# Down projection of a SwiGLU FFN by seven block products in place of eight, with the FFN's pools laid out anew

## The chip, the cores and the metric

One core of one Trainium2 chip runs the whole kernel. The metric is the device time of one execution in microseconds (us); the time before is the median of three runs. The profile is one further execution, taken by the hardware profiler.

## What is computed

One decoder layer on 512 tokens of 1024 features: a norm, a mixing stage with two groups of heads, a projection with residual, then the FFN (2816 inner features) and a last norm. The change lies in the FFN:

```python
h = rmsnorm(x, norm_ffn_w[l])
x = x + (jax.nn.silu(h @ w_gate[l]) * (h @ w_up[l])) @ w_down[l]
...
return rmsnorm(x, final_norm_w)
```

All of it is float32. The kernel gets float32 accuracy out of the matmul type float32r by splitting each operand into a head (`hi`, the value rounded to float32r) and a rest (`lo`), and by three matmuls in place of one (`mm3`): hi times hi, hi times lo, lo times hi.

## The kernel before

**Stages.** The first 278 us or so hold the projections and the attention; the output projection (`project`) and the norm before the FFN (`ffn_norm`, `norm_turn`, `norm_keep`) end them. Then come 22 blocks of 128 inner features. `gate_up(f)` multiplies one block of the gate and one of the up weights with the normed tokens: per weight 8 feature rows by `mm3`, 24 matmuls of 128x512, into one PSUM bank each (tag `G`, 4 banks). `gate_act(f)` takes Silu of the gate bank on ScalarE (L653), multiplies it with the up bank on VectorE (L654), and splits the product into `act` head and rest (L76 on ScalarE, L73 on VectorE).

**Down projection before.** `FFN_GROUPS = (12, 10)`: after 12 blocks, and again after the last 10, the loop over `hf` (two halves of the 1024 output columns) takes weight units of two blocks by 512 columns, and multiplies them for four tiles of 128 tokens into four banks (tag `D`); a bank is added to the residual `x2` at L742 when its sum is whole. The four last units are done token tile by token tile, so that tiles end one after the other.

**Weights.** `load_raw` loads a unit of 512 KB (tag `wr`, 3 buffers) from SyncE's queue, `split` makes the head (`copy_a`, L76, ScalarE) and the rest (`sub`, L73, VectorE) in one buffer (tag `ws`, 4 buffers). Of a block both weights are split some two blocks ahead of their use.

**The end.** For each token tile `rstd_halves` sums squares of both column halves on ScalarE (L154) and adds them on VectorE (L156, L158), GpSimd takes the power (L159), and both halves are scaled (L748, L749, L751) and stored.

**Order.** Each engine works through its own list in order. A scheduler writes the lists when the kernel is built; waits between engines are by semaphores. `last_norm` holds the splits of block 1 behind the last norm's rest.

Of the kernel before, what the change touches and what calls it, by code (L numbers as in the profile page):

```python
# [32 lines left out]
FFN_GROUPS = (12, 10)  # L33
# [3 lines left out]
NBIG, NP, NRAW, NSPL, T4, T2 = 11, 3, 3, 4, 3, 4  # L37


@with_exitstack  # L40
def hybrid_gmlp_nsa_kernel(
# [63 lines left out]
    def mm3(ps, sh, sl, mh, ml, first, last):  # L105
        nc.tensor.matmul(ps, lhsT=sh, rhs=mh, start=first, stop=False)  # L106
        nc.tensor.matmul(ps, lhsT=sh, rhs=ml, start=False, stop=False)  # L107
        nc.tensor.matmul(ps, lhsT=sl, rhs=mh, start=False, stop=last)  # L108
# [181 lines left out]
    # compressed blocks: rows (parity, d), columns (head, block)  # L290
# [18 lines left out]
    # compression MLPs, a quarter of the first layer at a time  # L309
# [61 lines left out]
    # keys, values, queries  # L371
# [106 lines left out]
    # =================== attention ===================  # L478
# [10 lines left out]
    # output projection  # L489
# [29 lines left out]
    # scores, a head at a time; groups of four heads share a tile of probabilities  # L519
# [32 lines left out]
    # compressed branch  # L552
# [34 lines left out]
    # probabilities times values: units of 128 keys, four heads  # L587
# [59 lines left out]

    acts = []

    def gate_act(f):  # L650
        pg, b = gu.pop(f)[1], f if f < FFN_GROUPS[0] else f - FFN_GROUPS[0]
        sg = t2([P, S], F32, f"sg{f}")
        nc.scalar.activation(sg, pg[0], AF.Silu)  # L653
        nc.vector.tensor_tensor(out=sg, in0=pg[1], in1=sg, op=OP.mult)  # L654
        if b % 2 == 0:
            if b // 2 < NP:
                acts.append(bp.tile([P, 2, 2, S], F32R, tag="P", name=f"act{f}", bufs=NP))
            else:
                acts.append(b8([P, 2, 2, S], F32R, f"act{f}"))
        at = acts[-1][:, b % 2]  # L660
        copy_a(at[:, 0], sg)
        sub(at[:, 1], sg, at[:, 0])

    # gate and up, a block of 128 features; the first in two halves of the tokens
    gu = {}

    def gate_up(f, part=None):
        if not part:
            ws = [load_cols(w, 0, KD, f * P, P, f"w{'gu'[a]}{f}", spare=f == 0, behind=last_norm if f == 1 else None)
                  for a, w in ((0, w_gate), (1, w_up))]  # L670
            gu[f] = ws, [bank("G" if part is None else "S", [P, S], f"gu{f}{a}") for a in range(2)]
        cut = slice(0, S) if part is None else slice(part * 256, part * 256 + 256)
        for (hi, lo), z in zip(*gu[f]):
            for k in range(KD):
                mm3(z[:, cut], hi[:, k], lo[:, k], h2h[k // 4][:, k % 4, cut], h2l[k // 4][:, k % 4, cut],
                    k == 0, k == KD - 1)
# [29 lines left out]
    gate_up(0, 1)  # L706
    gate_act(0)
    zp.__exit__(None, None, None)

    # =================== FFN ===================  # L710
    fp = tc.tile_pool(name="ps_f", bufs=1, space=PSUM, reuse_waits="tile")
    ps = fp.__enter__()
    f0 = 0
    onw = None
    for gi, nb in enumerate(FFN_GROUPS):
        last_group = gi == len(FFN_GROUPS) - 1
        if gi > 0:
            acts.clear()
        for b in range(nb):
            f = f0 + b  # L720
# [5 lines left out]
        for hf in range(2):
            c = slice(hf * 512, hf * 512 + 512)
            pd = [bank("D", [P, 512], f"pd{gi}{hf}{t}") for t in range(NT)]
            units = [load_cols(w_down, (f0 + b) * P, 2, hf * 512, 512, f"wd{gi}{hf}{b}") for b in range(0, nb, 2)]
            tail = NSPL if last_group and hf == 1 else 1  # L730
            chunks = [[u] for u in range(len(units) - tail)] + [list(range(len(units) - tail, len(units)))]
            for us in chunks:
                for t in range(NT):
                    ts = slice(t * P, (t + 1) * P)
                    for u in us:
                        hi, lo = units[u]
                        for k in range(2):
                            b = 2 * u + k
                            at = acts[u][:, k]
                            mm3(pd[t], at[:, 0, ts], at[:, 1, ts], hi[:, k], lo[:, k], b == 0, b == nb - 1)  # L740
            for t in range(NT):
                nc.vector.tensor_tensor(out=x2[t][:, c], in0=pd[t], in1=x2[t][:, c], op=OP.add)  # L742
# [42 lines left out]
```

## Time and profile before

| | us |
|---|---|
| median of 3 runs | 641.55 (640.45 to 644.6) |
| span of the profiled execution, first to last instruction | 639.6 |
| TensorE busy in it | 620.8 |
| VectorE busy | 315.2 |
| ScalarE busy | 267.6 |

The profiled execution has no time of its own beside its span; the median is 1.95 us over the span. PE is TensorE's matmuls, DVE VectorE, ACT ScalarE, POOL GpSimd, SP SyncE with its DMA queue. Matmuls overlap each other, so the time of a stretch over the number of its matmuls tells their pace, not the duration of one.

### The profile page before, as it was taken

The numbers are of one execution on the slowest core, as the hardware profiler recorded it, in microseconds if no ns is written. First come the engines' busy times: TensorE is split into PE (matmuls) and PEld (weight loads), VectorE is DVE, ScalarE is ACT, GpSimd is POOL, SyncE is SP. The second block draws the span as 40 slices with busy tenths as digits, with TensorE's granted clock in tenths as the row PEclk, the third lists the DMA queues.
The fourth block names the chain that finished last, engine by engine and source line by source line (L and its number), as shares of the span: only waits on it lengthen the run. The fifth ranks groups of instructions, "written<-read, shape, count | busy, mean of one in ns | idle before, by whom it ended". The sixth has DMA issues, their size and how long they took to land.

```text
span 639.6 us, 7644 instructions
## 1 busy us (share of the span) xinstructions
PE 620.8 (97%) x2913; PEld 503.6 (79%) x2913; DVE 315.2 (49%) x563; ACT 267.6 (42%) x489; POOL 67.3 (11%) x113
## 2 busy tenths in 40 slices
PE   7999899999999999999999999999999999999995
PEld 5778788787777667898888888888888888888884
DVE  4752778557878886753333333323233333333422
ACT  5753367467757775442222222211122222222322
POOL 3100100015533650100000000000000000000001
PEclk8999999999999999999999999999999999999999
DMA  8451535451000211043333333333323333333202
GB/s 311 144 138 56 176 107 166 155 184 48 1 2 20 79 44 56 2 132 99 98 99 98 99 98 99 98 100 98 96 82 100 89 99 96 99 99 99 66 34 98
DMA packets 76628, 61.85 MB, mean 97 GB/s; under 512 B 3872, under 2 KB 64304, under 8 KB 76592
## 3 DMA queue, kind: packets, MB, share of 16 engines
q1 hardware_dynamic: 76016, 60.32, 31.0%
q10 hardware_dynamic: 576, 1.05, 0.4%
q8 instruction: 23, 0.38, 0.2%
q14 instruction: 13, 0.11, 0.1%
HBM read 59.27 MB, written 2.10 MB: 96 GB/s over the span
## 4 chain that ended last, share of the span: by engine, by line
PE 88%; DVE 4%; ACT 3%; DMA 2%; POOL 1%; issue 1%; SPq 0%; POOLq 0%; ACTq 0%; DVEq 0%
PE gu L107 13%; PE gu L108 13%; PE gu L106 12%; PE pd L108 6%; PE pd L106 6%; PE pd L107 6%; PE o L618 4%; PE ptp L603 3%; PE s L535 2%; PE po L107 2%; PE po L108 2%; PE po L106 2%; PE z_v L108 1%; PE z_v L106 1%; PE z_v L107 1%; PE z_q L108 1%
## 5 line engine op out<-in xcount | busy, mean ns | idle before, releaser
L106 PE MATMUL gu<-h2h,wg_s 128*128 128x512 f32 (+1 forms) x184 | 70.1, 381 | 0.2 <-ACT h2h L76 0.2
L107 PE MATMUL gu<-h2l,wg_s 128*128 128x512 f32 (+1 forms) x184 | 70.0, 380 | 0.2 <-DVE h2l L73 0.2
L107 PE MATMUL gu<-h2l,wu_s 128*128 128x512 f32 (+1 forms) x184 | 69.9, 380 | 0.0
L108 PE MATMUL gu<-h2h,wu_s 128*128 128x512 f32 (+1 forms) x184 | 69.9, 380 | 0.0
L106 PE MATMUL gu<-h2h,wu_s 128*128 128x512 f32 (+1 forms) x184 | 69.9, 380 | 0.0
L108 PE MATMUL gu<-h2h,wg_s 128*128 128x512 f32 (+1 forms) x184 | 69.9, 380 | 0.0
L106 PE MATMUL pd<-wd_s,act 128*128 128x512 f32 x176 | 68.5, 389 | 0.0
L107 PE MATMUL pd<-wd_s,act 128*128 128x512 f32 x176 | 68.5, 389 | 0.0
L108 PE MATMUL pd<-wd_s,act 128*128 128x512 f32 x176 | 68.5, 389 | 0.0
L73 DVE TENSOR_TENSOR wg_s<-wg_r,wg_s 128x1024 fp32r<-128x1024 f32 x22 | 27.2, 1236 | 78.4 <-ACT wg_s L76 78.3
L76 ACT ACTIVATE wu_s<-wu_r 128x1024 fp32r<-128x1024 f32 x26 | 27.5, 1061 | 78.0 <-issue 63.1
L73 DVE TENSOR_TENSOR wd_s<-wd_r,wd_s 128x1024 fp32r<-128x1024 f32 x22 | 27.0, 1225 | 67.3 <-ACT wd_s L76 67.3
L76 ACT ACTIVATE wd_s<-wd_r 128x1024 fp32r<-128x1024 f32 x22 | 23.3, 1059 | 71.2 <-PE pd L108 43.7
L653 ACT ACTIVATE sg<-gu 128x512 f32<-128x512 f32 x22 | 13.2, 598 | 80.7 <-PE gu L108 80.7
L654 DVE TENSOR_TENSOR sg<-gu,sg 128x512 f32<-128x512 f32 x22 | 15.2, 692 | 57.0 <-PE gu L108 57.0
L107 PEld LDWEIGHTS gu<-h2l,wg_s 128*128 128x128 f32 x184 | 34.6, 188 | 7.0 <-DVE h2l L73 0.4
L106 PEld LDWEIGHTS gu<-h2h,wg_s 128*128 128x128 f32 x184 | 34.6, 188 | 7.0 <-ACT h2h L76 0.5
L159 POOL TENSOR_TENSOR rstd_y<-s_y,mhalf 128x1 f32<-128x1 f32 x4 | 2.2, 549 | 359.5 <-DVE s_y L158 359.5
L108 PEld LDWEIGHTS gu<-h2h,wu_s 128*128 128x128 f32 x184 | 34.6, 188 | 6.6
L107 PEld LDWEIGHTS gu<-h2l,wu_s 128*128 128x128 f32 x184 | 34.6, 188 | 6.6
L108 PEld LDWEIGHTS gu<-h2h,wg_s 128*128 128x128 f32 x184 | 34.6, 188 | 6.5
L106 PEld LDWEIGHTS gu<-h2h,wu_s 128*128 128x128 f32 x184 | 34.6, 188 | 6.4
(264 smaller groups left out, 1280.1 us busy)
## 6 DMA issues: line engine op xcount, KB each, us to landing
wg_r<-in_w_gate_dram SPq DMA_DIRECT2D x22, 512.0 KB, 3.9
wu_r<-in_w_up_dram SPq DMA_DIRECT2D x22, 512.0 KB, 3.7
wd_r<-in_w_down_dram SPq DMA_DIRECT2D x22, 512.0 KB, 3.7
wo_r<-in_w_o_dram SPq DMA_DIRECT2D x8, 512.0 KB, 4.3
x_sb<-in_x_dram SPq DMA_DIRECT2D x4, 512.0 KB, 9.1
wv_r<-in_w_in_dram SPq DMA_DIRECT2D x4, 512.0 KB, 7.7
wu_r<-in_w_in_dram SPq DMA_DIRECT2D x4, 512.0 KB, 3.7
w1k_r<-in_cmp_k_w_dram SPq DMA_DIRECT2D x4, 512.0 KB, 3.9
```

What stands on the lines that cost most here:

```text
L73: return (eng or nc.vector).tensor_tensor(out=o, in0=a, in1=hi.bitcast(F32), op=OP.subtract)
L76: return nc.scalar.activation(o, a, AF.Copy)
L106: nc.tensor.matmul(ps, lhsT=sh, rhs=mh, start=first, stop=False)
L107: nc.tensor.matmul(ps, lhsT=sh, rhs=ml, start=False, stop=False)
L108: nc.tensor.matmul(ps, lhsT=sl, rhs=mh, start=False, stop=last)
L159: nc.gpsimd.tensor_tensor(out=r, in0=ms[:, 1:2], in1=mhalf, op=OP.pow)
L535: nc.tensor.matmul(sb, lhsT=q, rhs=KAB[kv][:, a, b0:b0 + nbr, :n], start=(a == 0), stop=(a == 1))
L603: nc.tensor.transpose(pt[:rows, hh], src, ident)
L618: nc.tensor.matmul(o.rearrange("p h c -> p (h c)"), lhsT=v, rhs=PTs[u][:rows, a], start=(first and a == 0), stop=(last and a == 1))
L653: nc.scalar.activation(sg, pg[0], AF.Silu)
L654: nc.vector.tensor_tensor(out=sg, in0=pg[1], in1=sg, op=OP.mult)
```

## The change

Groups are now of 6, 6, 6 and 4 blocks. In a group, the blocks go in pairs (e = 0, 1). A pair's activations are four quarters: block e by half of the tokens; its down weights (256 rows by 1024 columns) are four quarters too: block e by half of the columns. The 2x2 by 2x2 product of quarters is done with seven products, M1 to M7, each on 2 token tiles (c) of 128: the operands of four of them are sums and differences of quarters, and banks `A`, `B`, `C` (two each) collect them; bank A goes through M1, M6, M7 and M4 and is added to a quarter of `x2` after each of them. A group's three pairs (two in the last) add into the same banks.

```diff
-FFN_GROUPS = (12, 10)
+FFN_GROUPS = (6, 6, 6, 4)
+NHALF, NDOWN = 8, 3
...
-    NB = {**dict(zip("MSTO", BANKS)), "G": 4, "D": 4}
+    NB = {**dict(zip("MSTO", BANKS)), "G": 2, "A": 2, "B": 2, "C": 2}
...
-    def split(raw, shape, name, eng=None, spare=False, behind=None):
+    def split(raw, shape, name, eng=None, spare=False, behind=None, halves=False):
...
+        elif halves:
+            hi = wp.tile([P, *shape], F32R, tag="wh", name=f"{name}_h", bufs=NHALF)
+            lo = wp.tile([P, *shape], F32R, tag="wh", name=f"{name}_l", bufs=NHALF)
...
     def gate_act(f):
+        pg, e = gu.pop(f)[1], f % 2
+        if e == 0:
+            raw_act[0] = t4([P, 4, 256], F32, f"sg{f}")
+        sg = raw_act[0]
+        own = sg[:, 2 * e:2 * e + 2].rearrange("p a c -> p (a c)")
+        nc.scalar.activation(own, pg[0], AF.Silu)
+        nc.vector.tensor_tensor(out=own, in0=pg[1], in1=own, op=OP.mult)
+        if e == 0:
+            return
+        ss = t4([P, 4, 256], F32, f"ss{f}")
+        ah, al = act_tile(f"ah{f}"), act_tile(f"al{f}")
+        copy_a(ah[:, 0:3], sg[:, 1:4])
+        for o, x, y, op in ((ss[:, 0], sg[:, 0], sg[:, 2], OP.add), (ss[:, 2], sg[:, 1], sg[:, 0], OP.subtract),
+                            (ss[:, 1], ss[:, 0], sg[:, 1], OP.subtract), (ss[:, 3], sg[:, 3], ss[:, 1], OP.subtract)):
+            nc.vector.tensor_tensor(out=o, in0=x, in1=y, op=op)
+        sub(al[:, 0:3], sg[:, 1:4], ah[:, 0:3])
+        copy_a(ah[:, 3:7], ss)
+        sub(al[:, 3:7], ss, ah[:, 3:7])
+        acts.append((ah, al))
...
     gate_up(0, 1)
+    for p in reversed(first_pools):
+        p.__exit__(None, None, None)
+    wp = ctx.enter_context(tc.tile_pool(name="weights_f", bufs=2, reuse_waits="tile"))
+    tp = ctx.enter_context(tc.tile_pool(name="temps_f", bufs=2, reuse_waits="tile"))
...
+    def down(gi, pairs):
+        raws = []
+        for p in pairs:
+            r = wp.tile([P, 2, 2, 512], F32, tag="wd", name=f"wd{p}_r", bufs=NDOWN)
+            nc.sync.dma_start(r, w_down[2 * p * P:(2 * p + 2) * P].rearrange("(e p) (h c) -> p e h c", p=P, h=2))
+            raws.append(r)
...
+        def product(name, slot, tag, first, src, before=None):
+            ws = []
+            for q, r in enumerate(raws):
+                if before:
+                    before(r)
+                w = wp.tile([P, 2, 512], F32R, tag="wh", name=f"wd{pairs[q]}{name}", bufs=NHALF)
+                b = src(r)
+                copy_a(w[:, 0], b)
+                sub(w[:, 1], b, w[:, 0])
+                ws.append(w)
+            for c in range(2):
+                if first:
+                    banks[tag, c] = bank(tag, [P, 512], f"p{tag}{gi}{c}")
+                z, ts = banks[tag, c], slice(c * P, (c + 1) * P)
+                for q, w in enumerate(ws):
+                    ah, al = acts[q]
+                    mm3(z, ah[:, slot, ts], al[:, slot, ts], w[:, 0], w[:, 1],
+                        first and q == 0, q == len(ws) - 1, not first)
...
+        product("M1", 0, "A", True, lambda r: r[:, 0, 0])
+        for c in range(2):
+            accumulate(2 + c, 0, banks["A", c])
+        product("M5", 3, "C", True, lambda r: r[:, 0, 0], diffs)
+        for c in range(2):
+            accumulate(c, 1, banks["C", c])
+        product("M6", 4, "A", False, lambda r: r[:, 0, 0], t2_of)
...
+        product("M2", 2, "B", True, lambda r: r[:, 1, 0])
+        product("M7", 5, "A", False, lambda r: r[:, 0, 1])
+        product("M3", 6, "C", False, lambda r: r[:, 1, 1])
+        product("M4", 1, "A", False, lambda r: r[:, 1, 0], t4_of)
+        for c in range(2):
+            accumulate(c, 0, banks["A", c])
...
-    for t in range(NT):
-        y = t4([P, DM], F32, f"y{t}")
+    for t in (2, 3, 0, 1):
+        y = b8([P, DM], F32, f"y{t}")
         r = rstd_halves(x2[t], y, f"y{t}")
```

`accumulate(t, hf, src)` adds a bank to a half of the columns of `x2[t]` on VectorE (128x512). `diffs(r)` is one VectorE subtraction of 128x1024 in place, `t2_of` and `t4_of` one of 128x512 each. A group's down weights now come as whole pairs of 1 MB (tag `wd`, 3 buffers). The first pools are closed before block 0's activation, and new pools take their memory.

How the lists stand now, at three places.

VectorE around the start of the first down projection. Before, `sg` is the Silu product of the last block, `wd_s` a weight unit, `act` the activation's rest, and `x_...<-pd` the addition to the residual:

```order
L654 TENSOR_TENSOR sg_3445<-gu_3396,sg_3445 128x512
L73 TENSOR_TENSOR wd_s<-wd_r,wd_s 128x1024
L73 TENSOR_TENSOR act_3382<-sg_3445,act_3382 128x512
L73 TENSOR_TENSOR wd_s<-wd_r,wd_s 128x1024 x5
L742 TENSOR_TENSOR x_0_1171<-pd_3450,x_0_1171 128x512
L742 TENSOR_TENSOR x_0_1171<-pd_3451,x_0_1171 128x512
```

Now, where wd0 to wd2 with M and a number are the weights of pairs 0 to 2 for one product (the first two here are M6's of pairs 0 and 1, wd2M_3174 is M6's of pair 2), `ss` the sums of quarters, and `al` the activation's rest:

```order
L675 TENSOR_TENSOR sg_3016<-gu_3032,sg_3016 128x512
L76 TENSOR_TENSOR wd0M_3166<-wd_r,wd0M_3166 128x512
L683 TENSOR_TENSOR ss_3083<-sg_3016 128x256
L76 TENSOR_TENSOR wd1M_3170<-wd_r,wd1M_3170 128x512
L683 TENSOR_TENSOR ss_3083<-ss_3083,sg_3016 128x256
L76 TENSOR_TENSOR al_3085<-sg_3016,ah_3084 128x768
L683 TENSOR_TENSOR ss_3083<-sg_3016,ss_3083 128x256
L76 TENSOR_TENSOR wd2M_3174<-wd_r,wd2M_3174 128x512
L748 TENSOR_TENSOR x_1_1172<-pA_3109,x_1_1172 128x512
L76 TENSOR_TENSOR al_3085<-ss_3083,ah_3084 128x1024
L748 TENSOR_TENSOR x_1_1172<-pA_3119,x_1_1172 128x512
```

The weight rests of a later product, three sums and the first addition to the residual now stand among the steps that the last pair's activations go through.

VectorE at the end of the program. Before, the last three additions and what stands behind them (`s_y`, `rstd_y` and `y` belong to the last norm of a token tile):

```order
L742 TENSOR_TENSOR x_1_1172<-pd_4626,x_1_1172 128x512
L158 TENSOR_TENSOR s_y_4803<-s_y_4803 128x1
L751 SCALAR_TENSOR_TENSOR y_4803<-x_1_1172,rstd_y_4808,onw 128x512
L742 TENSOR_TENSOR x_1_1172<-pd_4627,x_1_1172 128x512
L158 TENSOR_TENSOR s_y_4817<-s_y_4817 128x1
L751 SCALAR_TENSOR_TENSOR y_4816<-x_1_1172,rstd_y_4821,onw 128x512
```

Now, from the last addition on (tiles come in the order 2, 3, 0, 1; y_5057 is tile 3, y_5070 tile 0, y_5083 tile 1):

```order
L748 TENSOR_TENSOR x_0_1171<-pA_4905,x_0_1171 128x512
L166 TENSOR_TENSOR s_y_5058<-s_y_5058 128x1
L827 TENSOR_TENSOR y_5057<-x_1_1172,onw 128x512
L830 SCALAR_TENSOR_TENSOR y_5057<-x_1_1172,rstd_y_5062,onw 128x512
L164 TENSOR_SCALAR s_y_5071<-s_y_5071 128x1
L827 TENSOR_TENSOR y_5070<-x_0_1171,onw 128x512
L166 TENSOR_TENSOR s_y_5071<-s_y_5071 128x1
L164 TENSOR_SCALAR s_y_5084<-s_y_5084 128x1
L827 TENSOR_TENSOR y_5083<-x_0_1171,onw 128x512
L830 SCALAR_TENSOR_TENSOR y_5070<-x_0_1171,rstd_y_5075,onw 128x512
L166 TENSOR_TENSOR s_y_5084<-s_y_5084 128x1
L830 SCALAR_TENSOR_TENSOR y_5083<-x_0_1171,rstd_y_5088,onw 128x512
```

Behind the last addition there stood two rows, and now there stand eleven: three products with the norm's weight (L827), three scalings (L830) and five small rows of 128x1.

SyncE's queue around the first FFN weights. Before:

```order
L84 DMA wg_r<-in_w_gate_dram 128x8x128
L84 DMA wu_r<-in_w_up_dram 128x8x128
L84 DMA wg_r<-in_w_gate_dram 128x8x128
L84 DMA wu_r<-in_w_up_dram 128x8x128
L84 DMA wg_r<-in_w_gate_dram 128x8x128
L112 DMA onw<-in_final_norm_w_dram 128x1024
```

Now, from the same row on:

```order
L87 DMA wg_r<-in_w_gate_dram 128x8x128
L87 DMA wu_r<-in_w_up_dram 128x8x128
L120 DMA onw<-in_final_norm_w_dram 128x1024
L87 DMA wg_r<-in_w_gate_dram 128x8x128
L87 DMA wu_r<-in_w_up_dram 128x8x128
L87 DMA wg_r<-in_w_gate_dram 128x8x128
L756 DMA wd_r<-in_w_down_dram 128x2x1024
```

The last norm's weight (`onw`) has moved ahead of the loads of blocks 1 and 2, and the first pair of down weights stands behind them.

On TensorE the list is the same up to block 1 and has 66 matmuls of 128x512 fewer from there on; on VectorE it has 702 rows in place of 521, on ScalarE 398 in place of 328.

## Rows read from the trace of the kernel before

**Rows 1.** The page, its span and part 1: busy time, share, instructions.
```profile
span 639.6 us, 7644 instructions
...
PE 620.8 (97%) x2913; PEld 503.6 (79%) x2913; DVE 315.2 (49%) x563; ACT 267.6 (42%) x489; POOL 67.3 (11%) x113
```

**Rows 2.** The chain that ended last, around the FFN: start us, us, engine, tile, line.
```profile
278.60 0.39 PE gu L107
632.59 0.70 DVE x L742
```

**Rows 3.** Busy time of each engine from block 1 to the last matmul.
```profile
284.20:632.60 348.40, 348.36 (x1538) 288.12 (x1536) 118.31 (x135) 93.30 (x121) 1.65 (x3) 1.00 0.32 95
```

**Rows 4.** Groups by shape, 278 to 636 us: count | busy us, mean ns.
```profile
L106 PE MATMUL pd<-wd_s,act 128*128 128x512 f32 x176 | 68.5, 389 | 0.0
...
L106 PE MATMUL gu<-h2h,wg_s 128*128 128x512 f32 x168 | 65.4, 389 | 0.0
...
L73 DVE TENSOR_TENSOR wd_s<-wd_r,wd_s 128x1024 fp32r<-128x1024 f32 x22 | 27.0, 1225 | 67.3 <-ACT wd_s L76 67.3
...
L76 ACT ACTIVATE wd_s<-wd_r 128x1024 fp32r<-128x1024 f32 x22 | 23.3, 1059 | 71.2 <-PE pd L108 43.7 <-issue 27.5
...
L654 DVE TENSOR_TENSOR sg<-gu,sg 128x512 f32<-128x512 f32 x22 | 15.2, 692 | 57.0 <-PE gu L108 57.0
L73 DVE TENSOR_TENSOR act<-sg,act 128x512 fp32r<-128x512 f32 x22 | 15.1, 685 | 0.0
L76 ACT ACTIVATE act<-sg 128x512 fp32r<-128x512 f32 x22 | 13.6, 617 | 0.0
...
L742 DVE TENSOR_TENSOR x<-pd,x 128x512 f32<-128x512 f32 x16 | 10.7, 687 | 12.1 <-PE pd L108 12.1
```

**Rows 5.** Groups by shape, VectorE, whole span: one of 256 columns.
```profile
L572 DVE TENSOR_TENSOR sc<-ptc,cmask 128x256 f32<-128x256 f32 x4 | 1.7, 419 | 1.8 <-PE ptc L568 1.8
```

**Rows 6.** Timeline, VectorE, end of the first down half: start us, us [idle before].
```profile
433.55 1.28 DVE L742 TENSOR_TENSOR x<-pd,x 128x512 f32<-128x512 f32 x2
435.39 0.69 DVE L742 TENSOR_TENSOR x<-pd,x 128x512 f32<-128x512 f32 x1 [0.56 <-PE pd L108]
```

**Rows 7.** Timeline, VectorE, two scalings in a row.
```profile
273.24 1.42 DVE L166 SCALAR_TENSOR_TENSOR xf<-x,rstd_f,fwb 128x512 f32<-128x512 f32 x2 [0.66 <-POOL rstd_f L159]
```

**Rows 8.** Timeline, SyncE's queue, the last loads before the FFN.
```profile
247.01 0.37 SPq L84 DMA_DIRECT2D wg_r<-in_w_gate_dram  x1
274.68 0.34 SPq L112 DMA_DIRECT2D onw<-in_final_norm_w_dram  x1
```

**Rows 9.** DMA issues: count, KB each, median us to landing.
```profile
x_sb<-in_x_dram SPq DMA_DIRECT2D x4, 512.0 KB, 9.1
...
x<-in_x_dram SPq DMA_DIRECT2D x4, 512.0 KB, 6.8
```

**Rows 10.** Timeline, TensorE, the first matmul of block 1.
```profile
284.21 0.40 PE L106 MATMUL gu<-h2h,wg_s 128*128 128x512 f32 x1
```

**Rows 11.** Timeline, all engines, the end of the program.
```profile
632.17 0.39 PE L108 MATMUL pd<-wd_s,act 128*128 128x512 f32 x1
632.59 0.69 DVE L742 TENSOR_TENSOR x<-pd,x 128x512 f32<-128x512 f32 x1 [2.32 <-PE pd L108]
633.32 0.63 ACT L154 ACTIVATE y<-x 128x512 f32<-128x512 f32 x1 [3.07 <-DVE x L742]
...
634.07 0.16 DVE L158 TENSOR_TENSOR s_y<-s_y 128x1 f32<-128x1 f32 x1 [0.79 <-ACT y L154]
634.38 0.55 POOL L159 TENSOR_TENSOR rstd_y<-s_y,mhalf 128x1 f32<-128x1 f32 x1 [4.89 <-DVE s_y L158]
...
634.96 0.75 DVE L751 SCALAR_TENSOR_TENSOR y<-x,rstd_y,onw 128x512 f32<-128x512 f32 x1 [0.73 <-POOL rstd_y L159]
635.71 0.37 ACTq L750 DMA_DIRECT2D out_dram<-y  x1
```

More of the change, by code (lines that the diff above doesn't have):

```diff
@@ L55, in hybrid_gmlp_nsa_kernel @@
     bp = ctx.enter_context(tc.tile_pool(name="big", bufs=NBIG))
-    wp = ctx.enter_context(tc.tile_pool(name="weights", bufs=2))
-    tp = ctx.enter_context(tc.tile_pool(name="temps", bufs=3))
-    sp = ctx.enter_context(tc.tile_pool(name="small", bufs=4))
+    first_pools = [tc.tile_pool(name="weights", bufs=2), tc.tile_pool(name="temps", bufs=3),
+                   tc.tile_pool(name="small", bufs=4)]
+    wp, tp, sp = [p.__enter__() for p in first_pools]
     def b8(shape, dt, name):
         return bp.tile(shape, dt, tag="b8", name=name)
+    n_t4 = T4
     def t4(shape, dt, name):
-        return tp.tile(shape, dt, tag="t4", name=name, bufs=T4)
+        return tp.tile(shape, dt, tag="t4", name=name, bufs=n_t4)
     def t2(shape, dt, name):
@@ L103, in after, with mm3 @@
                           mybir.DependencyInfo(mybir.DependencyClass.NoSync, mybir.DependencyReason.DATA), reason="order")
[L105 to L108, printed above, removed]
+    def mm3(ps, sh, sl, mh, ml, first, last, more=False):
+        nc.tensor.matmul(ps, lhsT=sh, rhs=mh, start=first, stop=False, skip_group_check=more)
+        nc.tensor.matmul(ps, lhsT=sh, rhs=ml, start=False, stop=False, skip_group_check=more)
+        nc.tensor.matmul(ps, lhsT=sl, rhs=mh, start=False, stop=last, skip_group_check=more)
     def bcast_row(vec, n, name, tag=None):
@@ L648, in hybrid_gmlp_nsa_kernel, with act_tile @@
     acts = []
-    def gate_act(f):
[L651 to L662, printed above, removed]
+    n_act = [0]
+    raw_act = [None]
+    def act_tile(name):
+        n_act[0] += 1
+        if (n_act[0] - 1) % 8 < NP:
+            return bp.tile([P, 7, 256], F32R, tag="P", name=name, bufs=NP)
+        return b8([P, 7, 256], F32R, name)
+    def gate_act(f):
+        pg, e = gu.pop(f)[1], f % 2
[17 more added lines that the diff above has]
+        acts.append((ah, al))
     gu = {}
@@ L668, in gate_up @@
         if not part:
-            ws = [load_cols(w, 0, KD, f * P, P, f"w{'gu'[a]}{f}", spare=f == 0, behind=last_norm if f == 1 else None)
+            ws = [load_cols(w, 0, KD, f * P, P, f"w{'gu'[a]}{f}", spare=f == 0, behind=last_norm if f == 1 else None,
+                            halves=f > 0)
                   for a, w in ((0, w_gate), (1, w_up))]
@@ L706, in hybrid_gmlp_nsa_kernel @@
     gate_up(0, 1)
+    for p in reversed(first_pools):
+        p.__exit__(None, None, None)
+    wp = ctx.enter_context(tc.tile_pool(name="weights_f", bufs=2, reuse_waits="tile"))
+    tp = ctx.enter_context(tc.tile_pool(name="temps_f", bufs=2, reuse_waits="tile"))
+    sp = ctx.enter_context(tc.tile_pool(name="small_f", bufs=4, reuse_waits="tile"))
+    n_t4 = 2
     gate_act(0)
@@ L715, in hybrid_gmlp_nsa_kernel @@
     for gi, nb in enumerate(FFN_GROUPS):
[L716 to L720, printed above, removed]
+        acts.clear()
+        for f in range(f0, f0 + nb):
             if f > 0:
@@ L723, in hybrid_gmlp_nsa_kernel @@
                 gate_act(f)
-        if last_group:
+        if gi == len(FFN_GROUPS) - 1:
             onw = bcast_row(final_norm_w, DM, "onw", tag="wb")
[L726 to L732, printed above, removed]
-                for t in range(NT):
[L734 to L742, printed above, removed]
+        down(gi, range(f0 // 2, (f0 + nb) // 2))
         f0 += nb
-    for t in range(NT):
-        y = t4([P, DM], F32, f"y{t}")
+    for t in (2, 3, 0, 1):
+        y = b8([P, DM], F32, f"y{t}")
         r = rstd_halves(x2[t], y, f"y{t}")
```

28 lines of the change are left out of this document (24 added, 4 removed).

## Prediction

> **What bounds the kernel now.** I read the page's busy times first: TensorE is busy for 620.8 of 639.6 us, VectorE for 315.2 and ScalarE for 267.6 [rows 1]. The chain of waits then shows where that matters: from 278.60 it stays on TensorE's gate and up products and the down products and leaves them at 632.59 for the last norm [rows 2]. The windows give the stage's pace: from block 1's first matmul to the last one's end 348.40 us, all of them busy [rows 3]. Those are 6 x 168 gate and up matmuls and 3 x 176 down matmuls [rows 4], 1536 in all, so 348.40 / 1536 = 226.8 ns each; the 389 ns of a single one hold its overlap with the next. VectorE works for 118.31 us there, ScalarE for 93.30 [rows 3]. So in this stage a matmul less is 226.8 ns less, as long as operands come in time, and VectorE is a third used.
>
> **Matmuls removed.** Before, 22 blocks x 4 token tiles x 2 column halves x 3 = 528. Now a pair takes 7 products x 2 tiles x 3 = 42, and 11 pairs 462. 66 x 226.8 ns = 15.0 us, certain by the lists. Gate and up stay.
>
> **VectorE's new work in a down projection.** For a group of three pairs: 21 weight rests of 128x512, at 685 ns like the activation's (14.4 us); 3 differences of 128x1024 at 1225 (3.7); 6 of 128x512 (4.1); 14 additions at 687 (9.6) [rows 4]. That is 31.8 us, while TensorE needs 126 x 0.2268 = 28.6. But by the list 6 rests, 3 wide and 3 narrow differences (9.9 us) stand ahead of the last block's Silu product, under gate and up matmuls. In their place come the last pair's own steps: product 0.69, four sums of 128x256 at 0.42 [rows 5], rests of 768 columns (0.96, between 685 and 1225 ns) and 1024 (1.23), 4.6 in all; and the next block's two weight rests, 2.5. So 29.0 at full price. Two independent rows back to back take 1.28 us, not 1.37 [rows 6], which over some 40 rows is 3 us less: about 26. Between 26 and 29 against 28.6 is tight, but not late; I take the row of pairs, as most neighbours in the list are independent. ScalarE has 21 heads at 0.62 [rows 4] and is not near.
>
> [...]
>
> **Start of a down projection.** Call 0 the start of M1's first matmul. The last up matmul ends at about 0.16 (it started 0.23 before and lasts 0.39), and the product of Silu and up is done at about 0.9. Ahead of the copy of the activation's head on ScalarE stand the heads of M6's weights for pairs 0 and 1, whose buffers are those of the last block's up weight (a ring of eight, two blocks long), so they start only as this block ends: 2 x 0.62, until 1.1. The head of 768 columns (0.84, between 617 and 1059) is done at 1.9 to 2.3. TensorE reaches it after 8 matmuls, at 1.8: 0.1 to 0.5 us late. The rest of 768 columns comes, by VectorE's list, behind two weight rests and two sums: 3.7 to 4.1, and is wanted 8 matmuls later, at 3.8 to 4.1. The rest of 1024 follows after a sum, a weight rest and an addition: 6.5 to 7.0, wanted by the 29th matmul at 6.5 to 6.8. So 0.1 to 0.7 us for a group; I take 0.4, as the steps are late by about as much as the overlap of rows takes off. Four groups: 1.6 us. Before, the first chunk hid these steps: VectorE's last activation rest had 24 matmuls of other units ahead of it.
>
> Later products are fed: M6's last addition stands at about 14.5 in VectorE's list at full price, its bank is wanted for M7's second tile at about 19; M4's last weight rest is done at 23.5 and wanted at 26.5. The next block's weights are done at 26.6, wanted at 29.2. This holds with additions waiting for their bank as in the row of 0.56 us [rows 6].
>
> **The end.** Before, from the last matmul's end at 632.56 (632.17 and 0.39) the addition, square, power and scaling take until 635.71: 3.15 us [rows 11]. Now tiles 0 and 1 both end with M4, 3 matmuls apart, and VectorE, behind M4's last weight rest and tile 2's and 3's rows, has just finished the last addition but one when the last matmul ends. Behind it stand: scaling 0.67 (half of 1.42 [rows 7]), addition 0.60, small 0.11, product 0.60, scaling 0.67, small 0.11, product 0.60, two small 0.22, product 0.60, scaling 0.67, small 0.15, power 0.55 with 0.1 of handing over on either side, scaling 0.75: 6.5 us. So the tail is 3.4 us longer; 2.4 if VectorE is a microsecond ahead, 5 at full price with waits for the power.
>
> **The front.** The last norm's weight now stands ahead of block 1's loads on SyncE's queue. It waited until 274.68 in the trace, for the buffer that the FFN norm's weight leaves, while the loads up to 247.01 were long out [rows 8]. So block 1's gate weight leaves at 275.1. Queued loads of 512 KB landed in 6.8 us (four together) and 9.1 (at the start of the program) [rows 9]; as the second of four I take 5.5 to 6.8, that is by 281.9. Head 1.06 and rest 1.23 make 284.2; block 1 starts at 284.21 [rows 10], and its third matmul, at 284.66, is the first to want the rest. Cost 0; if it took the 9.1, 2 us.
>
> G has two banks instead of four: Silu frees the gate bank 0.6 us after the last gate matmul, plus a head of 1.06 ahead of it on ScalarE, and the next block wants it after 24 up matmuls, 5.4 us. No cost. The down loads of 1 MB a pair move the same bytes as before, a block or more ahead.
>
> **Sum.** -15.0 + 1.6 + 3.4 + 0 = -10.0 us on the profiled execution, 639.6 to 629.6. On the median, 1.95 over that span, 641.55 - 10.0 = 631.6.
>
> **Rivals.** First, nearly all of the gain stays: the starts cost 0.1 each, and the bare addition of tile 1 sets the tail, 1 us longer. 641.55 - 15.0 + 0.4 + 1.0 = 628.0. The lists speak for it, TensorE's rows of M1 to M6 being interleaved in the last group; eleven rows behind the last addition speak against it.
>
> Second, VectorE paces the down projection, and the kernel gets slower. In its list additions that wait for TensorE stand ahead of weight rests that TensorE wants two products on, and bank A must be read before M6, M7 and M4 may write it. At full price (29.0) plus five of the 14 additions waiting 0.6 us [rows 6], a group takes 32.0 in place of 28.6; the last one, with 16.5 + 4.6 at full price and 2 of waits, 23 in place of 19.0. That is 3 x 3.4 + 4 = 14.2 us: with the starts and the tail 641.55 - 15.0 + 14.2 + 1.6 + 3.4 = 645.8. It decides from the point where VectorE's list is 3 to 4 us later than I have it; at half of that the time is 638.7. A third of use in the whole stage [rows 3] speaks against it, the down stage's own 26 to 29 of 28.6 for it.
>
> [...]
>
> Third, the front or the two G banks hold up TensorE: if Silu or the product came 5.4 us late, each further us would cost 21 us over 21 blocks; the front alone 2. About 636 with a front of 2 us and a stall of 2 to 3 elsewhere.
>
> **How the numbers follow.** Forecast 0.60, range 629 to 634 (starts 0.4 to 2.8, tail 2.4 to 5); first rival 0.14; second 0.18, a good half of it at the half way of 638.7; third 0.08. Since unknown costs lie mostly above, the range is 627.5 to 639.5. A difference of 1%, 6.4 us, is about what can be told: faster means below 635.1. From the forecast nearly all, the first rival, and a little of the others: 0.76; same 0.19; slower 0.05.
>
> **What would show it.** In the profile after: 1470 matmuls from block 1 on at 226.8 ns; at each group's start TensorE idle in two or three gaps of 0.1 to 0.5 us, released by ScalarE's head or VectorE's rest of the activations; no gaps later in a group; between the last matmul and the last scaling 6 to 7 us of VectorE; block 1 not waiting for a DMA. Wrong it would be if TensorE waited for weight rests or additions in the middle of a group, or if the tail stayed at 3 us.

## The result and the profile after

| | before | after |
|---|---|---|
| median, us | 641.61 (640.45 to 644.6, 4 runs) | 631.36 (630.81 to 632.05, 4 runs) |
| ratio | | 0.9835, 95% interval 0.9813 to 0.9857 |
| span of the profiled execution, us | 639.6 | 629.2 |
| block 1's first matmul to the last one's end, us | 348.35 | 335.00 |
| from there to the end of the last scaling, us | 3.15 | 7.27 |

The forecast was 631.6. One of the executions of `e2_vector_one` below ran at a lower granted clock (0.85, 684.01 us) and is left out of its median. The two lower lines of the table come from the timeline: before, 284.21 to 632.56, and on to 635.71 [rows 10, 11]; after, 282.81 to 617.81, and on to 625.08.

The page's span and busy times of the changed kernel answer to [rows 1]:

```profile
span 629.2 us, 7754 instructions
...
PE 606.5 (96%) x2847; PEld 489.9 (78%) x2847; DVE 411.3 (65%) x735; ACT 298.7 (47%) x544; POOL 68.1 (11%) x113
```

VectorE works 96 us more than before, in 172 rows more, TensorE 14 us less. The windows show where that stands. Columns: stretch, then busy us and count for PE, PEld, DVE, ACT and POOL, then the granted clock, DMA share and GB/s. The stretches are the whole stage (as [rows 3]), the first group's down projection, the last group's, and the end:

```profile
282.81:617.81 335.00, 335.00 (x1472) 275.06 (x1470) 212.55 (x299) 122.74 (x172) 0.55 (x1) 1.00 0.31 95
337.24:365.90 28.66, 28.66 (x126) 23.31 (x125) 26.14 (x40) 13.99 (x20) 0.00 (x0) 1.00 0.31 106
598.04:617.81 19.77, 19.77 (x85) 15.30 (x83) 18.85 (x34) 9.92 (x21) 0.55 (x1) 1.00 0.00 0
617.81:629.20 11.39, 0.00 (x0) 0.00 (x0) 5.72 (x14) 4.82 (x10) 2.47 (x3) 0.66 0.49 184
```

Read three things in them. The granted clock is 1.00 of full speed over the stage, and in both down projections. The stage holds 1470 matmuls (the window counts two more, which block 0 began and which still run at its left edge, as in [rows 3]); at 226.8 ns each they need 333.4 us, and 1.6 us are left for waits. And VectorE, a third used over the stage before, is busy for 26.14 of 28.66 us in a three-pair group and for 18.85 of 19.77 in the last one. The 40 rows of the three-pair group last 29.0 us when their durations are added up one by one; neighbours overlap, and so the engine is busy for 26.14.

The durations that the sum took from neighbours [rows 4, 5] can now be read as they are, in the groups by shape of the stage (count | busy us, mean ns):

```profile
L748 DVE TENSOR_TENSOR x<-pA,x 128x512 f32<-128x512 f32 x31 | 21.2, 688 | 4.1 <-PE pA L116 3.7
...
L76 DVE TENSOR_TENSOR al<-sg,ah 128x768 fp32r<-128x768 f32 x11 | 10.4, 950 | 0.0
...
L683 DVE TENSOR_TENSOR ss<-sg 128x256 f32<-128x256 f32 x22 | 9.3, 422 | 0.4
```

A start of a down projection, from the timeline of the first group (start us, us, engine, line, operation, tiles):

```profile
337.24 0.39 PE L114 MATMUL pA<-wd0M,ah 128*128 128x512 f32 x1
337.44 0.69 DVE L675 TENSOR_TENSOR sg<-gu,sg 128x512 f32<-128x512 f32 x1 [2.25 <-PE gu L116]
...
338.28 0.83 ACT L79 ACTIVATE ah<-sg 128x768 fp32r<-128x768 f32 x1
...
338.83 0.39 PE L115 MATMUL pA<-wd0M,ah 128*128 128x512 f32 x1
...
339.16 0.50 PE L114 MATMUL pA<-wd2M,ah 128*128 128x512 f32 x1
339.50 0.39 PE L115 MATMUL pA<-wd2M,ah 128*128 128x512 f32 x1
...
342.52 1.23 DVE L76 TENSOR_TENSOR al<-ss,ah 128x1024 fp32r<-128x1024 f32 x1
...
343.63 0.39 PE L115 MATMUL pC<-wd0M,ah 128*128 128x512 f32 x1
...
343.86 0.44 PE L116 MATMUL pC<-wd2M,al 128*128 128x512 f32 x1
344.14 0.39 PE L116 MATMUL pC<-wd0M,al 128*128 128x512 f32 x1
```

The step from 338.83 to 339.16 is 0.33 us in place of 0.23: the head of the last pair's activations (`ah`) is done at 339.11. The step after it is 0.34 as well: the matmul behind the gap takes 0.50 instead of 0.39 and pushes the next one. At 344.14 another 0.05 goes, just behind the first matmul (343.86) that reads the rest of 1024 columns, done at 343.75. From 337.24 to the start of the 37th matmul it is 8.51 us where 36 x 0.2268 make 8.16: 0.35 lost per group.

The end, from the timeline of all engines, answers to [rows 11]:

```profile
617.42 0.39 PE L116 MATMUL pA<-wd10M,al 128*128 128x512 f32 x1
...
618.46 0.68 DVE L748 TENSOR_TENSOR x<-pA,x 128x512 f32<-128x512 f32 x1
...
619.13 0.68 DVE L827 TENSOR_TENSOR y<-x,onw 128x512 f32<-128x512 f32 x1
...
619.29 0.93 POOL L167 TENSOR_TENSOR rstd_y<-s_y,mhalf 128x1 f32<-128x1 f32 x1 [1.53 <-DVE s_y L166]
...
620.25 0.75 DVE L830 SCALAR_TENSOR_TENSOR y<-x,rstd_y,onw 128x512 f32<-128x512 f32 x1 [0.44 <-POOL rstd_y L167]
...
621.72 0.68 DVE L827 TENSOR_TENSOR y<-x,onw 128x512 f32<-128x512 f32 x1
621.82 0.99 POOL L167 TENSOR_TENSOR rstd_y<-s_y,mhalf 128x1 f32<-128x1 f32 x1 [1.60 <-DVE s_y L164]
...
622.84 0.75 DVE L830 SCALAR_TENSOR_TENSOR y<-x,rstd_y,onw 128x512 f32<-128x512 f32 x1 [0.44 <-POOL rstd_y L167]
...
623.74 0.55 POOL L167 TENSOR_TENSOR rstd_y<-s_y,mhalf 128x1 f32<-128x1 f32 x1 [0.94 <-DVE s_y L166]
...
624.33 0.75 DVE L830 SCALAR_TENSOR_TENSOR y<-x,rstd_y,onw 128x512 f32<-128x512 f32 x1 [0.66 <-POOL rstd_y L167]
625.08 0.37 ACTq L829 DMA_DIRECT2D out_dram<-y  x1
```

The last addition starts 0.65 us after the last matmul's end, and eleven rows stand behind it. Look at the two powers on GpSimd that took 0.93 and 0.99 us and not 0.55: each ends 0.41 us after the end of the product of `x` and `onw` that VectorE began just before (619.81 and 622.40). VectorE then waits 0.44 us for each of them.

### The profile page after: what moved, and what is told of

Same layout as the page of the kernel before. It is cut to its first block, busy times and chain, and to the rows that moved or that the text cites. A ratio compares the mean times of both kernels' runs of the same rounds, so it can differ in the third digit from the quotient of the medians.

```text
span 629.2 us, 7754 instructions
## 1 busy us (share of the span) xinstructions
PE 606.5 (96%) x2847; PEld 489.9 (78%) x2847; DVE 411.3 (65%) x735; ACT 298.7 (47%) x544; POOL 68.1 (11%) x113
## 4 chain that ended last, share of the span: by engine, by line
PE 87%; DVE 5%; DMA 2%; ACT 2%; POOL 1%; issue 1%; SPq 0%; POOLq 0%; ACTq 0%; DVEq 0%
PE gu L115 13%; PE gu L116 13%; PE gu L114 13%; PE o L626 4%; PE pA L114 3%; PE ptp L611 3%; PE pA L115 3%; PE pA L116 3%; PE s L543 2%; PE po L115 2%; PE po L116 2%; PE po L114 2%; PE pC L114 2%; PE pC L116 2%; PE pC L115 2%; PE z_v L116 1%
## 5 line engine op out<-in xcount | busy, mean ns | idle before, releaser
L115 PE MATMUL gu<-h2l,wg_h 128*128 128x512 f32 x168 | 65.4, 389 | 0.0
L114 PE MATMUL gu<-h2h,wg_h 128*128 128x512 f32 x168 | 65.4, 389 | 0.0
L116 PE MATMUL gu<-h2h,wu_l 128*128 128x512 f32 x168 | 65.4, 389 | 0.0
L115 PE MATMUL gu<-h2l,wu_h 128*128 128x512 f32 x168 | 65.4, 389 | 0.0
L116 PE MATMUL gu<-h2h,wg_l 128*128 128x512 f32 x168 | 65.4, 389 | 0.0
L114 PE MATMUL gu<-h2h,wu_h 128*128 128x512 f32 x168 | 65.4, 389 | 0.0
L548 ACT ACTIVATE P<-P,nm 128x128 f32<-128x128 f32 (+3 forms) x64 | 35.5, 558 | 7.6 <-DVE nm L546 7.5
L114 PEld LDWEIGHTS gu<-h2h,wu_h 128*128 128x128 f32 x168 | 31.6, 188 | 6.6
L82 POOL TENSOR_SCALAR P<-P,sm 128x128 f32<-128x128 f32 (+3 forms) x64 | 33.6, 544 | 28.3 <-DVE sm L555 25.4
L76 DVE TENSOR_TENSOR PT<-ptp,PT 128x512 fp32r<-128x512 f32 (+1 forms) x48 | 31.8, 681 | 6.3 <-ACT PT L79 5.9
```

The source lines that it names most:

```text
L82: nc.gpsimd.tensor_scalar(out=o, in0=a, scalar1=s, scalar2=1.0, op0=OP.mult, op1=OP.mult)
L548: e = nc.scalar.activation(pr, pr, AF.Exp, bias=nm[b], scale=-1.0, accum_out=sm[b])
```

## The experiments

All are compared by three numbers: the stage (block 1's first matmul to the last one's end), the tail (from there to the end of the last scaling), and the median. The start-up before block 1 moves by more than a microsecond between executions of one kernel: the changed kernel was profiled twice, and block 1 began at 282.81 in the one and at 284.06 in the other. So stage plus tail tell small effects better than medians do. The ratio sets each kernel against executions of the kernel before in the same rounds, so it can be compared from line to line where the medians can't.

| kernel | stage | tail | sum | median, us | ratio to before, 95% interval |
|---|---|---|---|---|---|
| before | 348.35 | 3.15 | 351.50 | 641.61 | |
| after | 335.00 | 7.27 | 342.27 | 631.36 | 0.9835 (0.9813 to 0.9857) |
| e1_eighth | 349.93 | 6.67 | 356.60 | 646.22 | 1.0073 (1.0052 to 1.0093) |
| e2_vector_one | 339.19 | 6.99 | 346.18 | 635.11 | 0.9901 (0.9878 to 0.9924) |
| e3_vector_all | 351.68 | 6.77 | 358.45 | 647.48, one run | |
| e4_onw_late | 335.14 | 7.22 | 342.36 | 632.06 | 0.9852 (0.9836 to 0.9867) |
| e5_starts | 336.43 | 6.79 | 343.22 | 633.22 | 0.9856 (0.9826 to 0.9886) |
| e9_tail | 338.71 | 4.11 | 342.82 | 632.07 | 0.9840 (0.9809 to 0.9871) |
| e10_tail_pool | 335.92 | 4.61 | 340.53 | 629.95 | 0.9807 (0.9776 to 0.9838) |
| e11_all | 340.68 | 4.12 | 344.80 | 633.97 | 0.9876 (0.9840 to 0.9912) |
| e15_psum_w | 335.05 | 6.53 | 341.58 | 630.99 | 0.9842 (0.9819 to 0.9864) |
| e16_best | 335.21 | 5.08 | 340.29 | 631.19 | 0.9843 (0.9824 to 0.9863) |
| e17_tail_pool_5 | 336.02 | 4.59 | 340.61 | 628.98 | 0.9813 (0.9800 to 0.9827) |
| e18_after_5 | 335.13 | 7.21 | 342.34 | 631.71 | 0.9854 (0.9840 to 0.9869) |

**e1_eighth: the 66 matmuls put back.** M2's matmuls run twice, in every group; nothing else changes.

```diff
-                for q, w in enumerate(ws):
+                for again in range(2 if name == "M2" else 1):
+                    for q, w in enumerate(ws):
...
```

> M2 is computed twice in every group (66 matmuls more, the count of the kernel before; the second pass overwrites the first). Theory that TensorE's pace sets the down projection: +66 x 0.2268 = +15.0 us, 646.3 us, and the stretch from block 1's first matmul to the last one's end grows from 335.0 to 350.0. Rival that VectorE paces it: VectorE gets the time as slack, so the stretch grows by under 12 us and TensorE's idle time shrinks.

```profile
282.61:632.54 349.93, 349.93 (x1538) 287.52 (x1536) 215.06 (x300) 123.90 (x172) 0.55 (x1) 1.00 0.29 91
```

In its stage there are 1536 matmuls, as many as before, and 14.93 us more than in the changed kernel: 66 x 226.8 ns is 14.97. So the matmuls are worth their full pace, and what the layout, VectorE's work and the tail cost by themselves is the sum 356.6 against 351.5, 5.1 us.

**e2_vector_one and e3_vector_all: more work for VectorE.** The weight rests are computed twice: in e2 those of a group's first pair (28 rows more), in e3 all (77 more).

```diff
                 sub(w[:, 1], b, w[:, 0])
+                if q == 0:
+                    sub(w[:, 1], b, w[:, 0])
```

> The weight rest of the first pair is made twice in every product: 28 more VectorE rows of 128x512, 16.8 us at 0.60 each, five of each seven inside the down projection. VectorE was busy for 26.1 of 28.7 us there (18.9 of 19.8 in the last group). Theory that it has a little slack left: some 3 us more per group against 2.6 free, so +2 to +7 us in all, 633 to 638. Rival that VectorE already paces: the whole 4 x 3.0 us is paid, +12, 643. If it had wide slack: 0 to +1.

> Every weight rest is made twice: 77 more VectorE rows, some 9 us per group inside the down projection (6 in the last). Theory of little slack: VectorE becomes the bound, 35 in place of 28.7 us, so +20 to +30 us, 651 to 661, with TensorE waiting for VectorE's weight rests in the middle of the groups. Rival of wide slack: under +10.

TensorE's waits in the two (what waited, for what: us, times, longest), first all those of e2:

```profile
PE pA L115 <- DVE wd9M L76: 2.1, 1, 2.1
PE pC L115 <- DVE wd9M L76: 1.4, 1, 1.4
```

and the four longest of e3:

```profile
PE pA L115 <- DVE wd9M L76: 2.8, 2, 2.1
PE pA L115 <- DVE wd3M L76: 1.4, 1, 1.4
PE pA L115 <- DVE wd0M L76: 1.3, 1, 1.3
PE pA L115 <- DVE wd6M L76: 1.3, 1, 1.3
```

In e2 only the last group (pair 9's weights, `wd9M`) waits; the stage is 4.2 us longer, and 4.05 of it are there (23.82 in place of 19.77). The three-pair groups took in some 3 us each and grew by 0.04. In e3 every group waits, and the stage is 16.7 us longer, below what stood in the expectation: the last group 4.9 (610.29 to 634.99 in place of 19.77), each of the others about 3.9. Of the 21 doubled rests of a group 15 stand in the down projection itself, 9 us of VectorE at 0.60 each, so by this estimate a three-pair group has about 5 us to give before TensorE pays. The last has none.

**e4_onw_late: the load of the last norm's weight held back** until the last pair's activations are done.

```diff
...
+        if name == "onw":
+            after(d, acts[-1][2])
...
```

> The load of the last norm's weight goes back behind the loads of the last blocks, so block 1's weights are loaded early as in the kernel before. Theory that the front costs nothing: no change, 631.4 us within 1 us, and block 1's first matmul stands 6.4 us after the last norm's rest begins, as in both kernels. Rival that the late loads cost: 1 to 2 us less.

No difference: block 1 begins 6.36 us behind the start of the last feature tiles' rests in this kernel, in the changed one (282.81 behind 276.45) and before (284.21 behind 277.85). The first of those rests (`h2l`) in the chain that ended last, before and after (start us, us, engine, tile, line):

```profile
277.85 0.70 DVE h2l L73
```

```profile
276.45 0.70 DVE h2l L76
```

The timeline of the changed kernel shows why, and answers to [rows 8, 10]:

```profile
273.28 0.34 SPq L120 DMA_DIRECT2D onw<-in_final_norm_w_dram  x1
273.73 0.37 SPq L87 DMA_DIRECT2D wg_r<-in_w_gate_dram  x1
...
279.81 1.06 ACT L79 ACTIVATE wg_h<-wg_r 128x1024 fp32r<-128x1024 f32 x1 [2.90 <-DMA wg_r<-in_w_gate_dram]
280.90 1.23 DVE L76 TENSOR_TENSOR wg_l<-wg_r,wg_h 128x1024 fp32r<-128x1024 f32 x1 [3.16 <-ACT wg_h L79]
...
282.81 0.40 PE L114 MATMUL gu<-h2h,wg_h 128*128 128x512 f32 x1
```

Block 1's gate weight leaves at 273.73, ScalarE waits for it until 279.81, 6.1 us later, and its rest is done at 282.13, before TensorE comes to it.

**e5_starts: M6's weights behind the activations.**

```diff
...
+                steps = copy_a(w[:, 0], b), sub(w[:, 1], b, w[:, 0])
+                if name == "M6":
+                    for step, behind in zip(steps, held):
+                        after(step, behind)
```

> Heads and rests of M6's weights stand behind the last pair's activation head (ScalarE) and rest (VectorE) in every group, instead of ahead of or among them. Theory (the start of a down projection waits for these two steps because other rows stand ahead of them): the 0.35 us that a group's start lost goes to 0.1 or less, the stretch from block 1's first matmul to the last one's end falls from 335.0 to 333.7-334.3, the time by about 1 us to 630.2-630.8. Rival (the start waits for the chain of product, head and rest itself, whatever stands beside it): gaps stay, stretch 335.0, 631.4. If M6's rests then come late, a gap ahead of M6 and a stretch above 335.

Mostly the rival. Each three-pair group, from its first down matmul to the next gate matmul, takes 28.81 us in place of 28.91: 0.1 of the 0.35 was the order, the rest is the chain of product, head and first matmul itself. In the last group (21.51 us in place of 19.77) the moved rows made VectorE late for the last product, and that cost more than the three starts gave. From its timeline, TensorE:

```profile
617.00 0.50 PE L115 MATMUL pA<-wd9M,ah 128*128 128x512 f32 x1 [0.92 <-DVE wd9M L76]
```

**e9_tail: the last norm ahead of the last product.**

```diff
...
+        if last:
+            m3()
         product("M2", 2, "B", True, lambda r: r[:, 1, 0])
...
+        if last:
+            for t in (2, 3):
+                norm_early(t)
+            for t in (2, 3):
+                norm_late(t)
...
         product("M4", 1, "A", False, lambda r: r[:, 1, 0], t4_of)
```

> In the last group the order of products is M1, M5, M6, M3, M2, M7, M4, so that tiles 2 and 3 are whole two products before the end and their norm is put ahead of M4's additions; of tiles 0 and 1 the finished column half is squared and multiplied with the norm's weight before M4 ends. Theory (the tail is 7.3 us because VectorE holds the rows of tiles 3, 0 and 1 behind the last addition): behind the last addition stand two small rows and two scalings, the last scaling ends 3.5 to 4.5 us after the last matmul, the time falls by about 3 us to 627.9-629. Rival (VectorE is the bound of the last group, and its total is unchanged): the rows put ahead of the last addition delay M4's weight rests, TensorE waits 1 to 3 us, the stretch grows from 335.0 to 336-338 and the time is 630 to 632.

The tail fell to 4.11, as the theory had it, but the stage grew by 3.7: the rival, and a little beyond its range (338.7, where it had 336 to 338). TensorE's rows with the two longest waits:

```profile
617.08 0.49 PE L114 MATMUL pA<-wd9M,ah 128*128 128x512 f32 x1 [1.51 <-DVE x L748]
...
620.21 0.50 PE L115 MATMUL pA<-wd10M,ah 128*128 128x512 f32 x1 [0.47 <-DVE wd10M L76]
```

The norm's rows pushed the addition that frees bank A, and M4's rests. What was behind the last matmul now stood ahead of it, and the sum stayed (342.82 against 342.27): in the last group VectorE's list is the bound, and order only says where it shows.

**e10_tail_pool: four rests of the last group on GpSimd**, on top of e9.

```diff
-                sub(w[:, 1], b, w[:, 0])
+                on_pool = gi == len(FFN_GROUPS) - 1 and (name, q) in (('M3', 1), ('M2', 1), ('M7', 1), ('M4', 1))
+                sub(w[:, 1], b, w[:, 0], nc.gpsimd if on_pool else None)
```

> As the run before it, with the weight rests of the second pair for M3, M2, M7 and M4 of the last group on GpSimd instead of VectorE (four rows of 128x512, 2.7 us less on VectorE). If the last group is bound by VectorE: no TensorE gap left in it, stretch 335.0, last scaling 3.5 us after the last matmul, 627.5-628.5; where the run before it had lost 1 to 3 us on TensorE, these come back. Rival (GpSimd is about twice as slow on a rest, 1.2 us each, and its rows come late): a gap ahead of the product it feeds, no better than the run before it.

The waits ahead of M4 are gone, the tail is 4.61. One wait remains, and its cause is new. From the timeline of all engines:

```profile
601.04 1.38 POOL L76 TENSOR_TENSOR wd10M<-wd_r,wd10M 128x512 fp32r<-128x512 f32 x1 [327.56 <-ACT wd10M L79]
...
601.18 1.51 DVE L683 TENSOR_TENSOR ss<-sg 128x256 f32<-128x256 f32 x1
...
602.62 0.94 DVE L76 TENSOR_TENSOR al<-sg,ah 128x768 fp32r<-128x768 f32 x1
...
603.62 0.73 PE L116 MATMUL pA<-wd10M,al 128*128 128x512 f32 x2 [0.49 <-DVE al L76]
```

A sum of 256 columns took 1.51 us, not 0.42: it ended 0.27 us behind GpSimd's rest (602.42). In e16 below, where that rest is back on VectorE, the same sum takes 0.42 again (599.25). The activation's rest came late by that, and TensorE waited. Two more VectorE rows beside a GpSimd rest (1.48 for 1.23 at 606.06, and 1.04 for 0.68 at 609.94) were held up. Of the 2.7 us that GpSimd took over, 2.3 are won on e9 (342.82 to 340.53), and 1.7 on the changed kernel.

**e11_all: e10 with e5's order**, M2's and M3's weights of the last group held as well.

> The run before it together with the starts' order. If the two are independent their gains add: 626.5-627.8 (stretch 333.7-334.3, last scaling 3.5 us after the last matmul). Rival (in the last group the held rows take the slack that the tail needs): 628 or more.

It lost 4.3 us on e10 (344.80 and 340.53). From GpSimd's timeline:

```profile
602.37 5.64 POOL L76 TENSOR_TENSOR wd10M<-wd_r,wd10M 128x512 fp32r<-128x512 f32 x3 [330.93 <-DVE x L750]
```

Three rests now stood in a row on GpSimd, 1.88 us each, where e10's four took 1.29 to 1.53; additions and rests came late through the last group (TensorE's waits of 0.65 us at 605.23, 0.42 at 607.52, 0.80 at 616.91 and 0.85 at 618.24). The two edits aren't independent. The granted clock was lower as well, 0.99 over the stage where the changed kernel has 1.00, and TensorE's pace fell: behind the waits at 616.91 and 618.24, a matmul between 619 and 621 us followed the one before it after 0.43 us in place of 0.23:

```profile
619.42 0.63 PE L116 MATMUL pA<-wd9M,al 128*128 128x512 f32 x1
619.85 0.63 PE L115 MATMUL pA<-wd9M,ah 128*128 128x512 f32 x1
```

It cost little, as the matmul at 621.90 had to wait for GpSimd's fourth rest, done at 621.84, at either pace.

**e15_psum_w: one operand of the norm's product in PSUM.**

```diff
...
+            onw_ps = bank("G", [P, 512], "onw_ps")
+            after(nc.scalar.copy(onw_ps, onw[:, 0:512]), held[0])
...
-        nc.vector.tensor_tensor(out=y[:, 0:512], in0=x2[t][:, 0:512], in1=onw[:, 0:512], op=OP.mult)
+        made = nc.vector.tensor_tensor(out=y[:, 0:512], in0=onw_ps, in1=x2[t][:, 0:512], op=OP.mult)
```

> The changed kernel with one operand of the last norm's product moved: half of the norm's weight is copied to a free PSUM bank, and the product reads it there, so that it has one operand in SBUF and not two. The order of VectorE's rows in the tail is held as it was. In the changed kernel the powers of tiles 3 and 0 on GpSimd, each beside such a product, took 0.93 and 0.99 us, the other two 0.55. Theory (a VectorE row with two operands in SBUF keeps GpSimd from its operands until it ends): all four powers 0.55, the last scaling ends 6.4 to 6.5 us after the last matmul in place of 7.27, 0.8 us off the time, about 630.5. Rival (the power is slow because its operand had just been written, or for a reason of GpSimd's own): powers stay at 0.93 and 0.99, tail 7.3.

From its timeline, a product and the power beside it:

```profile
622.01 0.68 DVE L830 TENSOR_TENSOR y<-onw_ps,x 128x512 f32<-128x512 f32 x1
622.11 0.55 POOL L169 TENSOR_TENSOR rstd_y<-s_y,mhalf 128x1 f32<-128x1 f32 x1 [1.53 <-DVE s_y L166]
...
622.70 0.75 DVE L841 SCALAR_TENSOR_TENSOR y<-x,rstd_y,onw 128x512 f32<-128x512 f32 x1
```

All four powers take 0.55, the scalings of tiles 3 and 0 no longer wait, and the tail is 6.53. The last addition starts 0.61 us behind the last matmul's end, where it was 0.65, so the tail begins as it did. The 0.7 us are below what the medians can tell; the trace shows them.

**e16_best: e10 mended** by order: M3's rests on VectorE and M4's weights ahead of the norm's rows; the three-pair groups have e5's order, and the small row of tile 1 stands ahead of tile 0's scaling.

```diff
...
+        w4 = weights("M4", lambda r: r[:, 1, 0], t4_of) if last else None
         add(((0, 1, "A"), (1, 1, "A")))
```

> The kernel with rests on GpSimd in its last group, mended where its trace showed waits: M3's rests stay on VectorE, behind the last pair's activation rest (the GpSimd one had held up a sum there, which took 1.51 us in place of 0.42); M4's differences and weights stand ahead of the norm's rows of tiles 2 and 3; the small row of tile 1 stands ahead of tile 0's scaling; in the groups of three pairs M6's weights stand behind the activation head and rest. Theory (every wait seen is one of order on VectorE or of GpSimd's rows beside VectorE's): the stretch from block 1 to the last matmul 334.2 to 335.0 (that kernel 336.2), the last scaling 3.6 to 4.2 us after it (4.6), the time 627.0 to 628.5. Rival (VectorE's total in the last group is the bound, whatever the order): the wait moves ahead of M4, whose bank is read by additions that now stand behind more rows; stretch 336 or more, no better than 629.5.

The stage is 0.7 us shorter than e10's and the tail 0.5 longer, so the sum is as good as the same, and neither the median nor the ratio is better. That is the rival in the time, though not in the stage, for which it had 336 or more. The wait has moved ahead of M4's first matmul, and GpSimd still holds VectorE up: a rest takes 1.78 us for 0.69 beside GpSimd's rest of 603.21, and a product 1.12 for 0.68 beside the one of 612.88; both end 0.55 us behind GpSimd's. From the timeline:

```profile
604.28 1.78 DVE L76 TENSOR_TENSOR wd10M<-wd_r,wd10M 128x512 fp32r<-128x512 f32 x1
...
613.84 1.12 DVE L763 TENSOR_TENSOR y<-x,onw 128x512 f32<-128x512 f32 x1
...
615.71 0.47 PE L114 MATMUL pA<-wd9M,ah 128*128 128x512 f32 x1 [0.66 <-DVE s_y L762]
```

**e17_tail_pool_5 and e18_after_5: e10 and the changed kernel side by side**, in five rounds on one chip.

> The kernel with four weight rests of the last group on GpSimd and the tail's norm put ahead, once more, in five rounds beside the changed kernel on the same chip. From block 1 to the last scaling its trace had 335.92 + 4.61 = 340.5 us, the changed kernel's 335.0 + 7.27 = 342.3. Theory (the 1.7 us are the whole difference between the two): 1.7 us less than the changed kernel. Rival (what separates the two medians so far, 631.4 and 630.0, is the scatter of the start): no difference.

> The changed kernel itself in five rounds, to stand beside the run before it: 631.4, stretch 335.0 and last scaling 7.3 us after the last matmul again, wherever block 1 starts.

628.98 against 631.71, with intervals of the ratio that don't touch (0.9800 to 0.9827 and 0.9840 to 0.9869). The sums differ by 1.73 us as expected; that the medians differ by 2.7 is more than the stage and the tail account for. So the version with the norm ahead and four rests on GpSimd is faster than both kernels.

## Why the prediction was right

**Matmuls, -15.0.** Right: 1470 of them at the old pace in the stage, and putting 66 back costs 14.93 (e1).

**Starts, 1.6.** Right in size: 0.35 us a three-pair group, 1.6 us of waits in the whole stage, first ScalarE's head and then, by 0.05, VectorE's rest. The forecast put them down to rows that stand ahead of the head and the rest; e5 shows that only 0.1 of 0.35 hangs on that.

**VectorE in a three-pair group, "about 26" of 28.6.** Right: 26.14. The overlap of neighbours [rows 6] decides it. The forecast's sum at full price, with no overlap, was 29.0. Single rows do last as long as it took them to (688 and 422 ns), and the 40 rows add up to 29.0; but independent rows of 512 columns back to back start 0.60 us apart (344.95 and 345.55).

**The front and the two G banks, 0.** Right: block 1 stands 6.36 us behind the last feature tile in both kernels, and e4 changes nothing. No gap of TensorE stands inside the gate and up matmuls, so the third rival fell as well.

**The tail, +3.4.** This is the term that was mis-sized: it measured +4.12 to the last scaling (7.27 for a forecast of 6.5). Behind it the last stores took 4.12 us, and 3.89 before; that 0.23 can't be told from scatter, as e4 with the same tail has 3.69. The step that failed was to count only one power, tile 1's ("power 0.55 with 0.1 of handing over on either side"), and no wait for those of tiles 3 and 0; only the upper bound of 5 had such waits. The 0.55 was read in a tail where nothing of VectorE's ran beside the power [rows 11]; here a product with two operands in SBUF did, and cost the powers 0.38 and 0.44. With that cause taken away the tail is 6.53 (e15), the forecast's 6.5. VectorE and GpSimd held each other up in both directions: a power beside that product, and in e10 a VectorE sum with two operands in SBUF beside a GpSimd rest (1.51 us in place of 0.42). Additions with one operand in PSUM beside a GpSimd rest kept their time (1.28 for two at 604.76 in e10, as in [rows 6]).

**The sum.** By the profiled executions: -13.35 in the stage and +4.12 behind it, -9.2 us. The span fell by 10.4, since block 1 also began 1.4 us earlier in this one execution; the repeated profile, at 284.06, shows that the changed kernel's start-up scatters by as much without any change. The five-round comparison has 640.96 against 631.71, -9.25. So the forecast of -10.0 was about 0.8 us too good, by the tail, and the first median, 0.24 us from the forecast, hid that by luck.

**The rivals.** The first (tail 1 us, starts 0.1) fell by the rows behind the last addition. The second, VectorE as the bound, did not happen in the three-pair groups, which have some 5 us to give (e3), but it is half true of the last group: with two pairs, no next block's idle time to run into, and the norm behind it, VectorE has no slack there (e2, e9). Its lateness came out as a longer tail and hardly as gaps: in M4 one matmul starts 0.06 us late behind a weight rest (615.36).

## What to carry to other kernels

When work moves from the bound engine to one with a third of use, take that engine's sum stage by stage: here three groups had room for all of it, the last, shorter one had none to spare, and what was left over came out behind the last matmul. A duration read where the other engines were quiet did not hold here with VectorE and GpSimd side by side: GpSimd's power of 0.55 us took 0.93 and 0.99 beside a VectorE product with two SBUF operands, and a VectorE sum of 0.42 took 1.51 beside a GpSimd rest. So look at what will run beside a row. And where a group is bound by one engine's total, reordering only moved the wait here (e9, and the last group of e5); taking rows away paid (e10, 2.3 us on e9), net of what the helper held up.

## What the hardware showed beyond that

A GpSimd rest of 128x512 took 1.29 and 1.30 us at its shortest (e10, at 609.14 and 605.16, beside additions that read PSUM) and 2.30 (e16, at 603.21) when a VectorE rest was there first (603.15). The other way round VectorE's row was done only behind GpSimd's, by 0.27 us for a sum that takes 0.42 otherwise and by 1.08 for a rest that takes 1.23 (e10, at 601.18 and 606.06). And a TensorE gap of a tenth of a microsecond cost twice at every start of a down projection of the changed kernel (339.16, 433.35, 527.54 and 599.96): the first matmul behind it lasts 0.50 us instead of 0.39, and the next one starts 0.33 to 0.34 us behind it instead of 0.23.
